# Loads of grouped keys and queries in pieces of 32 rows, in block 1's attention

## The chip, the cores and the metric

The kernel runs on one core of one Trainium2 chip. The metric is the device time of one execution in microseconds (us), as the median of several executions. Five engines work side by side, each through its own queue in order: TensorE (PE: matmuls, with the weight loads PEld), VectorE (DVE), ScalarE (ACT), GpSimd (POOL) and SyncE (SP), which in this stage issues all the loads and stores.

## The reference, cut to what matters

The program is a chain of three transformer blocks over 512 tokens of width 1024, all in float32. Only the first one's attention is touched. It has two kinds of heads: eight differential heads, whose query and key width is 32 twice over, and eight grouped-query heads of width 64, where four query heads share one key and value head.

```python
def gqa_attention(q, k, v):
    scale = d ** -0.5
    def block(qb):
        qg = qb.reshape(B, N_KV_B, GQA_GROUP, Q_BLOCK, d)
        s = jnp.einsum('bkgqd,bksd->bkgqs', qg, k) * scale
        p = jax.nn.softmax(s, axis=-1)
        o = jnp.einsum('bkgqs,bksd->bkgqd', p.astype(v.dtype), v)
...
qb = apply_rope(rms_norm(qb, q_norm), cos, sin)
kb = apply_rope(rms_norm(kb, k_norm), cos, sin)
ob = gqa_attention(qb, kb, vb)
x = x + jnp.concatenate([oa, ob], axis=-1) @ w_out
x = x + 0.5 * swiglu(rms_norm(x, ffn2_norm), ffn2_w_gate, ffn2_w_up, ffn2_w_down)
```

## The kernel before

All activations lie transposed: 128 partitions of features, 512 tokens in the free dimension. Float32 accuracy comes from splitting an operand into two parts, hi and lo, so a projection of 1024 x 128 weights is 24 matmuls of 128x512 (`mm3x`, L112; lines 116 to 118).

Block 1's attention is `heads1` (L559), called by `mix1` (L516). It runs the sixteen heads in an order written out by hand: differential head h, then grouped head h, for each chunk c of 0 to 3 and each r of 0 and 1. A head has four steps, one for each block of 128 queries. `attend` (L427) walks through all steps: in each it computes the scores and the exponentials of one step (`unit`, `soft`), turns and multiplies the weights of a step some way back (`values`, L455), and then takes one piece of "fill" (L724): a quarter of a projection for a later chunk (`proj_pieces`, L506), or, when those are used up, a piece of the first half of the output projection (`half_res`, L542). The fill keeps TensorE at work while DVE and ACT work on the softmax.

Queries and keys go through DRAM, because the heads need them in other partitions than the projection leaves them in. `parts` (L489) splits a projected chunk into hi and lo, and L500 stores both as one tile of 128 rows x 2 parts x 512 numbers (512 KB): `qdd` and `kdd` for the differential heads, `qpd` and `kpd` for the grouped ones. They are loaded back in three ways:

- `operand` (L614, load in L618) makes one stacked operand of a differential head: three loads of 32 partitions, 128 KB each, read as 32 rows by 2 heads. Tiles `qd` and `kd`.
- `keys` (L587, load in L592) makes the keys of a group of four heads: for the hi and the lo part one tile `kg`, of which both halves of 64 partitions get the same rows. That is four loads of 64 partitions, each read as 2 groups of 32 rows that lie 64 rows apart (`[(64, 2), (1, 32)]`).
- `ahead_gqa` (L683, load in L688) makes the queries of one grouped head: one tile `qg`, hi in the upper 64 partitions and lo in the lower, two loads of the same form.

`part_rows` (L503) writes the source's access pattern: row r and part i of such a tile begin at number 1024 r + 512 i, and each row read is 512 numbers long (2 KB).

The scores of a grouped head are two matmuls (L655): `qg` against the hi keys, then against the lo keys. Those of a differential head are one matmul for each of its two halves (L631).

`mk_diff` (L691) asks for the queries of the grouped head that follows, and `mk_gqa` (L695) for the operands of the differential head that follows, so each load is asked for about one head ahead. There are two buffers for `qg`, three for `kg` and four for `qd` and `kd` together. The order in which every engine gets its instructions is then worked out by a planner while the program is built (`schedule_with_timeline_sim=True` in `kernel`), from its own estimates of how long everything takes. SP issues its loads and stores in that order, and an issue that has to wait holds what is behind it.

Of the kernel before, what the change touches and what calls it, by code (L numbers as in the profile page):

```python
# [29 lines left out]
def f32v(ap):  # L30
    return ap.bitcast(F32)


class K:
    NU = 5
    SECOND = ("dq", "pf", "ct", "cacc")
    out = "out"
# [521 lines left out]
    def heads1(self, xhl, rb, gq, ind, ocs, rest):  # L559
        nc, D = self.nc, self.D  # L560
# [26 lines left out]
        def keys(kv):  # L587
            ds = []
            for i in range(2):
                t = self.keep("kg", 3, F32R)  # L590
                for r in range(2):
                    nc.sync.dma_start(out=f32v(t[64 * r:64 * r + 64]), in_=self.part_rows(gds[4], i, 32 * kv, [(64, 2), (1, 32)]))  # L592
                ds.append(t)
            return ds

# [65 lines left out]
        qds, kds, gds, ops = {}, {}, {}, {}  # L661
# [21 lines left out]
        def ahead_gqa(c, r):  # L683
            if r == 0 and c % 2 == 0:
                kg[c // 2] = keys(c // 2)
            t = self.keep("qg", 2, F32R)
            for i in range(2):
                nc.sync.dma_start(out=f32v(t[64 * i:64 * i + 64]), in_=self.part_rows(gds[c], i, 32 * r, [(64, 2), (1, 32)]))  # L688
            ops[4 + c, r] = t

        def mk_diff(c, r):  # L691
            ahead_gqa(c, r)
            return diff_head(2 * c + r, sms[c], *ops[c, r])
# [1434 lines left out]
```

## Time and profile before

| | us |
|---|---|
| median of 3 runs | 2696.18 (2693.70 to 2700.77) |
| the profiled execution, its own time | 2699.23 |
| its span, first to last instruction | 2697.5 |
| granted TensorE clock, mean over the span | 0.983 |
| block 1's attention, first load of an operand to last scores | about 404 to 681 |
| issues of `kg` (L592), 128 KB each | 8 |
| issues of `qg` (L688), 128 KB each | 16 |

In a row of the timeline stand the start and the length in us, the engine, the line, the operation, what it writes and reads, and in brackets how long the engine was idle before it and what ended that. "SPq" is SP's queue: its rows are the issues, not the transfers. In the chain of waits, a row such as "DMA kg<-kpd" is the time from an issue until what was waiting for the transfer went on. A row of the table by stages has the stretch, its length, the busy time of PE, PEld, DVE, ACT and POOL with the number of instructions, the granted clock of TensorE, the share of the 16 DMA engines' time that was busy, and GB/s.

### The profile page before, as it was taken

To read this page: it belongs to the slowest core of one execution; us is meant where nothing else is said; L and a number is where in the kernel's file an instruction comes from. 1 tells how busy PE (TensorE), PEld (TensorE's weight loads), DVE (VectorE), ACT (ScalarE), POOL (GpSimd) and SP (SyncE) were. 2 spreads that over 40 slices of the span, in tenths; PEclk is the share of its full clock that TensorE was granted. 3 is DMA by queue.
4 is the path that set the end of the run, shared out by engine and by line. 5 is a ranking of instruction groups with operands and counts; after the bars stand their busy time and mean duration, and the time that the engine had idled before them with its cause. 6 is when DMAs were issued, how large, how long until landed. Compare 5 with 4: busy or idle time off the path is not lost.

```text
span 2697.5 us, 31053 instructions
## 1 busy us (share of the span) xinstructions
PE 2606.5 (97%) x11752; PEld 2101.4 (78%) x11752; DVE 1579.3 (59%) x2435; ACT 1053.3 (39%) x1617; POOL 433.0 (16%) x343
## 2 busy tenths in 40 slices
PE   8999997899999999999999999999999899999999
PEld 6887785677788887888788877888778777878787
DVE  7866654777653554467434854434545977747464
ACT  4222234556422333455323443223433464424232
POOL 1011013433000001324111211000210313101000
PEclk9999998889999999999999999999999999999999
DMA  5566643334532233532223442222524634322333
GB/s 194 179 201 197 201 165 116 100 104 133 190 102 94 83 105 113 161 105 83 82 94 126 137 150 93 94 94 96 177 70 156 198 103 154 103 94 91 97 94 110
DMA packets 114449, 339.99 MB, mean 126 GB/s; under 512 B 13768, under 2 KB 15752, under 8 KB 114170
## 3 DMA queue, kind: packets, MB, share of 16 engines
q1 hardware_dynamic: 103866, 301.02, 34.4%
q0 software_dynamic: 10432, 36.97, 4.4%
q8 instruction: 92, 1.51, 0.2%
q14 instruction: 59, 0.48, 0.1%
HBM read 301.47 MB, written 40.67 MB: 127 GB/s over the span
## 4 chain that ended last, share of the span: by engine, by line
PE 87%; DVE 6%; DMA 4%; ACT 2%; issue 1%; POOL 0%; SPq 0%; DVEq 0%; POOLq 0%; ACTq 0%
PE b L118 5%; PE b L116 5%; PE b L117 5%; PE d L118 5%; PE d L116 5%; PE d L117 4%; PE f L116 4%; PE f L117 4%; PE f L118 4%; PE a L117 4%; PE a L118 4%; PE a L116 4%; PE c L116 4%; PE c L117 4%; PE c L118 4%; PE e L118 4%
## 5 line engine op out<-in xcount | busy, mean ns | idle before, releaser
L133 ACT ACTIVATE whi<-wraw 128x1024 fp32r<-128x1024 f32 (+3 forms) x419 | 423.7, 1014 | 1020.1 <-PE d L117 162.1
L134 DVE TENSOR_TENSOR wlo<-wraw,whi 128x1024 fp32r<-128x1024 f32 (+4 forms) x395 | 476.0, 1207 | 311.7 <-ACT whi L133 308.6
L116 PE MATMUL b<-xh,whi 128*128 128x512 f32 x360 | 141.9, 394 | 7.2 <-ACT xh L189 7.2
L118 PE MATMUL b<-xh,wlo 128*128 128x512 f32 x360 | 141.6, 393 | 0.4 <-DVE wlo L134 0.4
L117 PE MATMUL b<-xl,whi 128*128 128x512 f32 x360 | 141.8, 394 | 0.0
L118 PE MATMUL d<-xh,wlo 128*128 128x512 f32 x352 | 138.4, 393 | 2.0 <-DVE wlo L134 2.0
L116 PE MATMUL d<-xh,whi 128*128 128x512 f32 x352 | 138.6, 394 | 0.0
L117 PE MATMUL d<-xl,whi 128*128 128x512 f32 x352 | 138.0, 392 | 0.0
L118 PE MATMUL f<-xh,wlo 128*128 128x512 f32 x344 | 134.9, 392 | 0.6 <-DVE wlo L134 0.6
L116 PE MATMUL f<-xh,whi 128*128 128x512 f32 x344 | 135.2, 393 | 0.0
L117 PE MATMUL f<-xl,whi 128*128 128x512 f32 x344 | 134.3, 390 | 0.0
L186 ACT ACTIVATE hh<-h 128x512 fp32r<-128x512 f32 x98 | 61.8, 630 | 144.1 <-DVE h L365 92.6
L945 POOL TENSOR_TENSOR acc<-sq 128x512 f32<-128x512 f32 x10 | 14.1, 1410 | 641.1 <-ACT sq L292 375.8
L118 PE MATMUL e<-xh,wlo 128*128 128x512 f32 x288 | 112.9, 392 | 1.6 <-DVE wlo L134 1.6
L116 PE MATMUL e<-xh,whi 128*128 128x512 f32 x288 | 112.9, 392 | 0.0
L117 PE MATMUL c<-xl,whi 128*128 128x512 f32 x280 | 110.4, 394 | 2.6 <-DVE xl L190 2.6
L117 PE MATMUL e<-xl,whi 128*128 128x512 f32 x288 | 112.8, 392 | 0.0
L117 PE MATMUL a<-xl,whi 128*128 128x512 f32 x280 | 110.7, 395 | 2.0 <-DVE xl L190 2.0
L116 PE MATMUL a<-xh,whi 128*128 128x512 f32 x280 | 110.9, 396 | 0.0
L116 PE MATMUL c<-xh,whi 128*128 128x512 f32 x280 | 110.3, 394 | 0.3 <-ACT whi L133 0.3
L118 PE MATMUL a<-xh,wlo 128*128 128x512 f32 x280 | 110.2, 393 | 0.0
L118 PE MATMUL c<-xh,wlo 128*128 128x512 f32 x280 | 110.1, 393 | 0.0
(1178 smaller groups left out, 6510.2 us busy)
## 6 DMA issues: line engine op xcount, KB each, us to landing
wraw<-w_up SPq DMA_DIRECT2D x76, 512.0 KB
mw<-w_mod POOLq DMA_DIRECT2D x48, 512.0 KB, 4.5
wraw<-ffn_w_gate SPq DMA_DIRECT2D x43, 512.0 KB
wraw<-ffn_w_up SPq DMA_DIRECT2D x43, 512.0 KB
wraw<-w_down SPq DMA_DIRECT2D x40, 512.0 KB
wraw<-ffn_w_down SPq DMA_DIRECT2D x32, 448.0 KB
wraw<-w_gate SPq DMA_DIRECT2D x24, 512.0 KB
wraw<-ffn_w_down SPq DMA_DIRECT2D x16, 512.0 KB
```

The costliest lines, as they stand in the source:

```text
L116: mm(out, ah, bh, start=(first and i == 0), stop=False)
L117: mm(out, ah, bl, start=False, stop=False)
L118: self.last_mm = mm(out, al, bh, start=False, stop=(last and i == n - 1)).ins
L133: nc.scalar.activation(hi[:, i:j], raw[:, i:j], AF.Copy)
L134: (nc.gpsimd if self.pool_lo else nc.vector).tensor_sub(lo[:, i:j], raw[:, i:j], f32v(hi[:, i:j]))
L186: nc.scalar.activation(hi, x, AF.Copy)
L945: i = (self.nc.vector if c == 6 else self.nc.gpsimd).tensor_add(a, acc, s).ins
```

## The change

Each load of 64 partitions is cut into two of 32 partitions, which read the two groups of 32 rows one by one. The same bytes go to the same places. The 8 loads of `kg` become 16 and the 16 of `qg` become 32, of 64 KB each. The stores, the operand loads of the differential heads, the buffers and all the computation stay as they are.

```diff
@@ keys
                 t = self.keep("kg", 3, F32R)
                 for r in range(2):
-                    nc.sync.dma_start(out=f32v(t[64 * r:64 * r + 64]), in_=self.part_rows(gds[4], i, 32 * kv, [(64, 2), (1, 32)]))
+                    for a in range(2):
+                        nc.sync.dma_start(out=f32v(t[64 * r + 32 * a:64 * r + 32 * a + 32]), in_=self.part_rows(gds[4], i, 32 * kv + 64 * a, [(1, 32)]))
                 ds.append(t)
@@ ahead_gqa
             t = self.keep("qg", 2, F32R)
             for i in range(2):
-                nc.sync.dma_start(out=f32v(t[64 * i:64 * i + 64]), in_=self.part_rows(gds[c], i, 32 * r, [(64, 2), (1, 32)]))
+                for a in range(2):
+                    nc.sync.dma_start(out=f32v(t[64 * i + 32 * a:64 * i + 32 * a + 32]), in_=self.part_rows(gds[c], i, 32 * r + 64 * a, [(1, 32)]))
             ops[4 + c, r] = t
```

## The prediction

> **What bounds the kernel now.** I read the page first, then the table by stages over block 1's attention, then TensorE's waits there, and last the DMA queue's own order. The page's head:
>
> ```profile
> span 2697.5 us, 31053 instructions
> ...
> PE 2606.5 (97%) x11752; PEld 2101.4 (78%) x11752; DVE 1579.3 (59%) x2435; ACT 1053.3 (39%) x1617; POOL 433.0 (16%) x343
> ```
>
> TensorE is busy 97% of the span, so only the holes in its work can be won. Two stages of 62 and 58 us around the end of the attention (columns: length, busy time of PE, PEld, DVE, ACT, POOL, then the granted clock, the DMA share of 16 engines, GB/s):
>
> ```profile
> 570.00:632.00 62.00, 54.46 (x269) 42.76 (x268) 45.82 (x109) 37.95 (x83) 19.50 (x15) 0.89 0.31 90
> 632.00:690.00 58.00, 55.26 (x294) 42.07 (x292) 44.42 (x105) 36.88 (x82) 19.21 (x14) 1.00 0.38 124
> ```
>
> From 632 on PE is busy 55.26 of 58 us at clock 1.00, although DVE and ACT do as much there as in the 62 us before. The work pushed behind the attention's steps is a fixed amount, so an idle microsecond saved before 632 should come out at the end nearly whole. The holes that a DMA ends, from the timeline of PE (in brackets the idle time before it):
>
> ```profile
> 453.54 0.76 PE L655 MATMUL a<-kg,qg 128*128 128x512 f32 x1 [5.29 <-DMA kg<-kpd]
> 458.75 0.47 PE L655 MATMUL a<-kg,qg 128*128 128x512 f32 x1 [1.13 <-DMA kg<-kpd]
> 498.84 0.77 PE L631 MATMUL a<-kd,qd 96*128 96x512 f32 x1 [5.59 <-DMA kd<-kdd]
> 559.84 0.77 PE L631 MATMUL a<-kd,qd 96*128 96x512 f32 x1 [3.42 <-DMA qd<-qdd]
> 625.16 0.76 PE L631 MATMUL a<-kd,qd 96*128 96x512 f32 x1 [4.85 <-DMA qd<-qdd]
> ```
>
> These five waits are 5.29 + 1.13 + 5.59 + 3.42 + 4.85 = 20.28 us, and the table of waits lists no others there that a transfer ends for PE. I call them place 1 (453.54 and 458.75), place 2 (498.84), 3 (559.84) and 4 (625.16). Only place 1 names a tile that the change touches; places 2 to 4 wait for operands of the differential heads. What links them is in the chain of waits and in SP's queue (start, length, what):
>
> ```profile
> 441.65 4.14 DMA kpd<-hl
> 447.42 11.19 DMA kg<-kpd
> 484.62 6.72 DMA kdd<-hl
> 549.43 6.47 DMA kdd<-hl
> 557.32 2.51 DMA qd<-qdd
> 612.51 8.81 DMA kdd<-hl
> ```
>
> ```profile
> 445.80 6.97 SPq L592 DMA_DIRECT2D kg<-kpd  x6
> 478.72 1.04 SPq L688 DMA_DIRECT2D qg<-qpd  x2
> 485.53 0.50 SPq L688 DMA_DIRECT2D qg<-qpd  x1
> 491.40 1.26 SPq L618 DMA_DIRECT2D kd<-kdd  x3
> 494.11 4.34 SPq L618 DMA_DIRECT2D kd<-kdd  x3
> 541.98 1.04 SPq L688 DMA_DIRECT2D qg<-qpd  x2
> 555.96 1.26 SPq L618 DMA_DIRECT2D kd<-kdd  x3
> 607.11 1.04 SPq L688 DMA_DIRECT2D qg<-qpd  x2
> 621.34 1.26 SPq L618 DMA_DIRECT2D kd<-kdd  x3
> ```
>
> At places 2 to 4 the chain goes back through the operand loads to the store `kdd`, which takes 6.72, 6.47 and 8.81 us to land. Each of these stores stands behind two loads of `qg` in SP's order (478.72, 541.98, 607.11), and the `kd` loads of place 2 behind a third (485.53). The DMA share says why that matters; five stretches, the last with nothing but operand loads of 32 rows:
>
> ```profile
> 449.00:459.00 10.00, 4.33 (x11) 3.24 (x12) 0.00 (x0) 1.65 (x2) 0.45 (x1) 0.83 0.13 50
> 488.60:492.00 3.40, 3.40 (x14) 2.75 (x13) 0.51 (x1) 0.60 (x1) 0.00 (x0) 0.65 0.13 51
> 553.20:556.40 3.20, 2.99 (x14) 2.26 (x14) 2.03 (x4) 2.21 (x8) 0.00 (x0) 1.00 0.11 44
> 616.00:620.50 4.50, 3.33 (x15) 2.11 (x13) 3.02 (x6) 2.08 (x6) 0.00 (x0) 1.00 0.13 51
> 622.70:625.20 2.50, 0.04 (x1) 0.07 (x1) 0.00 (x0) 0.00 (x0) 0.00 (x0) 0.78 0.93 261
> ```
>
> In 449 to 459 only the `kg` loads run: share 0.13 at 50 GB/s. Two of 16 engines are 0.125, so one load of 64 rows (131 KB) runs on two engines and takes 131/50 = 2.6 us; four take 10.5, which is the 11.19 us of the chain at place 1. The same share appears as a tail at places 2 (488.6 to 492.0), 3 (553.2 to 556.4) and 4 (616.0 to 620.5): 14 engines have finished, and the store waits for its share on the two that the `qg` loads have filled. The operand loads, whose outermost extent is 32 on both sides, run at 0.93.
>
> **The change part by part.** 24 loads (8 of `kg`, 16 of `qg`) become 48 with the same bytes, each 32 rows on both sides. This trace has none of exactly that form. The nearest rows are the old loads and the operand loads (min, median, max ns of one issue):
>
> ```profile
> L592 SPq DMA_DIRECT2D kg<-kpd x8: 475/499/2443, 445.8 to 559.2; - x8
> ```
>
> ```profile
> L688 SPq DMA_DIRECT2D qg<-qpd x16: 474/496/879, 427.9 to 626.4; - x16
> ```
>
> ```profile
> L618 SPq DMA_DIRECT2D kd<-kdd x24: 302/423/536, 406.3 to 625.0; - x24
> ```
>
> *Issue.* I take 0.42 us from L618, the same outermost 32 rows; the other end is 0.50 from L592. SP goes from 24 x 0.50 = 12.0 to 48 x 0.42 = 20.2 us, 8.2 more over some 200 us. Behind the added issues at places 2 to 4 stand first-operand loads and the `kdd` store; I cost this at nothing, because between 485.53 and 491.40 and in the like gaps SP waits for that store. If that cover is gone, it is two issues, 0.84 us, at each of three places, 2.5 us.
>
> *Landing.* One operand load landed 2.51 us after its issue (557.32 above); I take that for a piece, although a piece has half the bytes. The far end is 4.14, a 512 KB store with little beside it (441.65).
>
> *Place 1.* The stored keys land at 445.80 and the loads start. The first operand becomes four pieces: the fourth starts 3 x 0.42 later, at 447.06, and lands at 449.6. PE then starts 3.9 us sooner than 453.54. The second operand's last piece is the eighth: 445.80 + 7 x 0.42 + 2.51 = 451.25. PE has 4.1 us of work between its two waits, to 453.7, so the 1.13 goes too: 5.0 together; 3.4 with 4.14 as landing.
>
> *Place 2.* With no two-engine queue ahead of it the store should land as the undisturbed one did, 484.62 + 4.14 = 488.76. From the first load of a group of three to PE's start pass 3.85 us (555.96 to 559.84 and 621.34 to 625.16 are 3.88 and 3.82), so the operands are there at 492.7, before PE runs dry at 498.84 - 5.59 = 493.25. All 5.6 us go. At the low end the store keeps its 6.72 us, and only 491.40 to 498.84 (7.44) shrinks to 3.85: 3.6 us.
>
> *Place 3.* 549.43 + 4.14 = 553.57 instead of 555.90: 2.3 us, the rest of the wait stays. Low end 0, if the store's own writing sets it.
>
> *Place 4.* By 616.0 the other 14 engines were done. The two `qg` loads, spread out, add 262 KB / 16 = 16 KB to each engine, 0.65 us at 25 GB/s; landing followed the tail's end by 0.8. So 617.5 instead of 621.3: 3.8 us.
>
> The sum of the waits is 5.0 + 5.6 + 2.3 + 3.8 = 16.7, between 3.4 + 3.6 + 0 + 3.8 = 10.8 and 20.3.
>
> *Clock.* After each of the four places PE runs at clock 0.50 (first 453.5 to 456.9, 3.40 us; the other three 6.80 us; columns as above):
>
> ```profile
> 497.80:504.60 6.80, 5.76 (x18) 4.84 (x19) 3.07 (x8) 2.60 (x6) 0.91 (x1) 0.50 0.48 141
> ...
> 624.10:630.90 6.80, 5.74 (x16) 4.61 (x17) 2.67 (x7) 2.75 (x6) 1.25 (x1) 0.50 0.53 125
> sum 23.80, PE 21.13 PEld 17.09 DVE 8.78 ACT 8.87 POOL 3.92; mean PE 5.28 PEld 4.27 DVE 2.19 ACT 2.22 POOL 0.98
> ```
>
> At full clock the 21.13 busy us would take half, so at most 10.6 are to be had. They are not all mine: a shorter gap was followed by half clock too, with 1.5 us of idle PE in 2.6,
>
> ```profile
> 485.00:487.60 2.60, 1.07 (x3) 0.68 (x4) 2.46 (x5) 1.95 (x6) 0.00 (x0) 1.00 0.85 302
> 487.60:491.00 3.40, 3.40 (x11) 2.73 (x10) 0.39 (x2) 0.30 (x3) 0.00 (x0) 0.50 0.38 124
> ```
>
> and places 1, 3 and 4 keep 1.0 to 1.4 us of idleness. I take a third, 3.5 us, between 0 and 10.6. The Trainium skill, TensorE: Matmul & The Clock Gate, Part 1, puts the drop after an idle window of about 3.4 us; by that, no wait that is left would bring it, and the sum would be 27 us. The trace speaks against it with the row above.
>
> Together 16.7 + 3.5 = 20.2 us. The profiled execution took 2699.23 us for its span of 2697.5 and lies 3.05 above the median of the runs, 2696.18; taken off that median it gives 2676. The order of all instructions is worked out by a planner from its own estimates; a load that it moves can give or take one such wait, up to 5.6 us, which the range holds.
>
> **The rivals.** *The stores are slow by themselves.* Then only place 1 (5.0) and the loads of place 2 (3.6) gain: 8.6 us, 2687.6. For it: writing 512 KB took 4.14 us even undisturbed. Against it: tails at 0.11 to 0.13 before each landing. Chance 0.15.
>
> *The pieces still go to two engines*, or what they free is hidden anyway: the same bytes at the same 50 GB/s, about 2696. Against it stands the 0.93 of loads with 32 rows outermost. The Trainium skill, DMA: Bandwidth & Descriptors, Why a DMA increments its semaphore by 16 and not by 1, gives the number of engines as the largest up to 16 that divides the outermost extents of both sides: 2 for 64 and 2, 16 for 32 and 32. The trace agrees as to the first, 0.13. Chance 0.09.
>
> *Slower: the pieces pay one after another.* SP takes its queue in order, and an issue can be held until an unrelated load has landed:
>
> ```profile
> SPq L618 <- DMA qg<-qpd: 4.7, 2, 3.1
> ```
>
> One `kg` issue took 2.443 us, and three `kd` issues at 494.11 took 4.34. If every piece waits 2.51 us for the one before, place 1's eight end at 445.80 + 20.1 = 465.9, 7.1 us later than now. At place 4 four query pieces take 10 us instead of 1.04; with the three operand loads between, the store starts 6.0 us later, at 618.5, and lands 4.14 later, 1.4 after today's 621.3. At places 2 to 4 alike that is 7.1 + 3 x 1.4 = 11.3 us: 2707.5. It decides from a spacing of (12.95 - 2.51)/7 = 1.5 us between pieces, where place 1 breaks even. Against it: operand loads stand 0.42 us apart in groups of three. The Trainium skill, DMA: Bandwidth & Descriptors, Rules for kernel authors, speaks for this outcome: it advises one large transfer over several small ones, and says that transfers to disjoint partition halves serialize on the same engines. Its ground, that both halves already use all 16, is not what the 0.13 shows. Chance 0.09.
>
> **How the numbers follow.** The forecast has 0.67. Its own range goes from 2696.2 - 30.9 (all waits and all of the clock) to 2696.2 - 10.8: 2665 to 2685. To hold the time 8 times in 10 the range takes in the first rival and a little for the planner: 2664 to 2690. What a measurement of this kernel can tell from no change is about 0.3%, 8.1 us, so faster means below 2688.1. Faster is 0.66 from the forecast and 0.09 from the first rival, 0.75; the same is 0.06 of the first, 0.08 of the second and 0.01 each of forecast and third, 0.16; slower 0.01 and 0.08, 0.09.
>
> **What would show it.** In the profile after, 48 issues at L593 and L690 of about 0.42 us; no stretch at share 0.13 after a store; `kdd` landing in 3 to 5 us; PE's DMA waits in the attention down from 20.3 to about 4 us; two or three half-clock stretches fewer; and from 632 on the same work, some 20 us earlier. The forecast is wrong if the tails at 0.13 remain (second rival), if they go and the stores still take 6 to 9 us (first), or if SP's issues of pieces last 1.5 us and more (third).

## The result, and the profile after

The changed kernel takes 2664.12 us (median of 4 executions, 2662.76 to 2667.01) against 2694.94 us of the kernel before (2690.91 to 2700.77). The ratio is 0.9885, with a 95% interval of 0.9865 to 0.9906: 31 us less, between 25 and 36. A ratio below 1 is faster. A second set of four executions gave 2667.23 us (expected 2662 to 2667), 0.9898 (0.9884 to 0.9913), and in its profile no hole is left in the attention that a DMA ends. The forecast was 2676, 20 us less, with a range of its own from 2665 to 2685; 2664.12 lies just under it.

The head of the page of the changed kernel:

```profile
span 2665.2 us, 31091 instructions
...
PE 2592.2 (97%) x11752; PEld 2090.8 (78%) x11752; DVE 1582.3 (59%) x2435; ACT 1051.9 (39%) x1617; POOL 431.8 (16%) x343
```

The span is 32.3 us shorter. PE's busy time went from 2606.5 to 2592.2 us with the same 11752 matmuls, 14.3 less, and its idle time from 2697.5 - 2606.5 = 91.0 to 2665.2 - 2592.2 = 73.0, 18.0 less. Both happened in the attention. The table by stages, from 425 us to the first load of the next block's context (688.02 before, 654.89 after), first of the kernel before, then of the changed one:

```profile
425.00:688.02 263.02, 225.15 (x1063) 172.17 (x1064) 182.00 (x423) 149.83 (x325) 93.91 (x65) 0.90 0.35 109
```

```profile
425.36:654.89 229.53, 210.09 (x1063) 161.33 (x1064) 184.88 (x423) 148.67 (x325) 93.89 (x65) 0.96 0.40 125
```

Same 1063 matmuls, 33.5 us less: 15.1 us less of busy time at a mean clock of 0.96 in place of 0.90, and 18.4 us less idleness (263.02 - 225.15 = 37.87, and 229.53 - 210.09 = 19.44). All of the gain arises here, and 32.3 of the 33.5 us are still there at the end.

The holes that a DMA ended were 20.28 us. In the changed kernel's timeline of PE only one is left. (From here on a line's number can be one to five higher than in the kernel before, where the edit added lines above it.)

```profile
483.86 0.47 PE L632 MATMUL a<-kd,qd 96*128 96x512 f32 x1 [1.16 <-DMA kd<-kdd]
```

The keys' and queries' loads (min, median, max ns of one issue):

```profile
L593 SPq DMA_DIRECT2D kg<-kpd x16: 317/419/423, 444.0 to 538.8; - x16
```

```profile
L690 SPq DMA_DIRECT2D qg<-qpd x32: 317/419/737, 428.3 to 596.1; - x32
```

SP's queue around the four places. The time from a store's row to the row of the load behind it is the store's landing:

```profile
441.42 0.32 SPq L500 DMA_DIRECT2D kpd<-hl  x1
444.03 5.42 SPq L593 DMA_DIRECT2D kg<-kpd  x12
475.67 0.34 SPq L500 DMA_DIRECT2D kdd<-hl  x1
478.70 1.27 SPq L619 DMA_DIRECT2D kd<-kdd  x3
531.71 0.34 SPq L500 DMA_DIRECT2D kdd<-hl  x1
534.66 1.26 SPq L619 DMA_DIRECT2D kd<-kdd  x3
586.13 0.32 SPq L500 DMA_DIRECT2D kdd<-hl  x1
590.61 1.26 SPq L619 DMA_DIRECT2D kd<-kdd  x3
```

The three `kdd` stores land after 3.0, 3.0 and 4.5 us, before it was 6.72, 6.47 and 8.81. The key store at 441.42 also lands sooner, after 2.6 us where it was 4.14. While the keys come in, PE no longer stops (stretch, length, busy time of PE, PEld, DVE, ACT, POOL, clock, DMA share, GB/s):

```profile
446.00:450.00 4.00, 4.00 (x25) 3.48 (x24) 1.29 (x2) 1.69 (x3) 0.17 (x1) 1.00 0.51 143
```

The share is 0.51 and not 0.13, and PE is busy 4.00 of 4 us. The first scores with the new keys start at 449.88 without a wait.

### The profile page after: what moved, and what is told of

It is laid out like the page before. It is cut to its first block, busy times and chain, and to the rows that moved or that the text cites. A ratio compares the mean times of both kernels' runs of the same rounds, so it can differ in the third digit from the quotient of the medians.

```text
span 2665.2 us, 31091 instructions
## 1 busy us (share of the span) xinstructions
PE 2592.2 (97%) x11752; PEld 2090.8 (78%) x11752; DVE 1582.3 (59%) x2435; ACT 1051.9 (39%) x1617; POOL 431.8 (16%) x343
## 4 chain that ended last, share of the span: by engine, by line
PE 79%; issue 8%; DVE 6%; DMA 3%; ACT 2%; POOL 1%; SPq 0%; POOLq 0%; DVEq 0%; ACTq 0%
PE d L118 4%; PE d L116 4%; PE b L118 4%; PE f L116 4%; PE d L117 4%; PE f L117 4%; PE b L116 4%; PE b L117 4%; PE f L118 4%; PE a L118 4%; PE a L117 4%; PE a L116 4%; PE c L116 3%; PE c L117 3%; PE c L118 3%
```

## The experiments

My theory is that of the forecast: a load whose outer extent (the count of its slowest dimension) is 2 runs on two DMA engines, and what stands behind it on those two is late. It has two rivals. A: smaller pieces land earlier, whatever engines they use. B: the planner's other order of instructions brought the gain. All ratios are to the kernel before on the same chip, with their 95% intervals.

**Whole loads, other order of reading** (twice). The two dimensions of the source change places; the loads stay whole. Queries and keys get the same permuted order of features, so the scores are the same sums. Every engine's instructions stand in the order of the kernel before.

```diff
-in_=self.part_rows(gds[4], i, 32 * kv, [(64, 2), (1, 32)])
+in_=self.part_rows(gds[4], i, 32 * kv, [(1, 32), (64, 2)])
...
-in_=self.part_rows(gds[c], i, 32 * r, [(64, 2), (1, 32)])
+in_=self.part_rows(gds[c], i, 32 * r, [(1, 32), (64, 2)])
```

> The 24 loads stay whole, 64 partitions each, but the source is read with the 32 rows as the outer extent and the two groups as the inner one, for keys and queries alike (both get the same permuted order of rows, so the scores are the same sums). Every engine's instructions stand in the same order as in the kernel before. Theory (a load whose outer extent is 2 on one side runs on two DMA engines, and what is behind it on those two waits): outer extents 32 and 64 use all 16, no stretch at a DMA share of 0.13, the kdd stores land in 3 to 4.5 us, PE's DMA waits in the attention 20.3 -> under 2 us, time 2660 to 2670. Rival A (smaller pieces land earlier, whatever engines they use): nothing is cut, so about 2695. Rival B (the planner's other order brought the gain): the order is that of before, so about 2695.

> The 24 whole loads with 32 rows as the outer extent once more, beside the others of this set: does the form without added issues beat the changed kernel? It saves 24 issues, of which two stand ahead of the first scores at place 1 (0.8 us). Theory: 2662 to 2668, not to be told from the changed kernel.

Measured: 2666.29 us, 0.9902 (0.9885 to 0.9919), and 2662.78 us, 0.9876 (0.9861 to 0.9891). The gain comes with no load cut and no instruction moved. This settles it against both rivals: neither the size of the pieces nor the planner's order is needed, only the outer extent. The second run's loads, a stretch in which only keys are loaded, and what PE still waits for in the attention (total us, times, longest):

```profile
L592 SPq DMA_DIRECT2D kg<-kpd x8: 518/594/597, 442.9 to 536.3; - x8
```

```profile
445.00:448.50 3.50, 3.50 (x22) 3.01 (x21) 1.29 (x2) 1.09 (x2) 0.00 (x1) 1.00 0.63 186
```

```profile
PE a L631 <- DMA kd<-kdd: 0.8, 1, 0.8
```

A share of 0.63 is the full time of ten engines, so more than eight are at work. This form needs 24 issues and not 48, but one takes 0.59 us and not 0.42. From the changed kernel (0.9885 and 0.9898) it can't be told apart.

**Pieces on 2, 4, 8 and 16 engines.** The 48 pieces of the change, but with their 32 rows read in two dimensions (2 by 16, 4 by 8, 8 by 4, 16 by 2), again alike for queries and keys. The four kernels have one and the same order of instructions on every engine.

```diff
-32 * kv + 64 * a, [(1, 32)])
+32 * kv + 64 * a, [(1, 2), (2, 16)])      # or (1, 4), (4, 8); (1, 8), (8, 4); (1, 16), (16, 2)
...
-32 * r + 64 * a, [(1, 32)])
+32 * r + 64 * a, [(1, 2), (2, 16)])
```

> The 48 loads of 32 partitions of the changed kernel, but each reads its 32 rows as 2 outer by 16 inner (rows 0, 2, 4 ... and then 1, 3, 5 ..., for keys and queries alike). Theory: each piece runs on two engines, 64 KB in 1.3 us; the tails at share 0.13 are back, PE waits about 20 us for DMAs, time 2690 to 2705, as before or a little slower for the 24 issues more. Rival A (smaller pieces by themselves): 2660 to 2670, as the changed kernel. Rival B (the planner's order): between, since its order is near that of the changed kernel: 2664 to 2680.

> The 48 pieces with their 32 rows read as 4 outer by 8 inner. Theory: four engines each, DMA share 0.25 where they run alone, 64 KB in 0.65 us at 100 GB/s; a query's tail is a quarter of that before, so most of the waits go: PE waits 2 to 6 us for DMAs, 2668 to 2678. If the count of engines did not matter, as with two engines, 2690 to 2700; if any count over two were as good as 16, 2662 to 2667.

> The 48 pieces with their 32 rows read as 8 outer by 4 inner. Theory: eight engines, 64 KB in 0.33 us, which is less than the 0.42 us of an issue, so nothing queues: 2662 to 2669, PE waits under 2 us.

> The 48 pieces with their 32 rows read as 16 outer by 2 inner: 16 engines. Every engine's instructions stand in the same order as in the kernels with 2, 4 and 8 engines, which is another order than that of the changed kernel. It tells the engines apart from the planner's order. If 16 engines are worth more than 8: 2664 to 2668, as the changed kernel. If the planner's order costs the rest: 2672 to 2677, as with 8 engines, and 8 us of the changed kernel's lead over those forms belong to its order.

| outer extent | median us | ratio | PE's DMA waits in the attention, us |
|---|---|---|---|
| 2 | 2695.89 | 1.0009 (1.0001 to 1.0018) | 18.7 |
| 4 | 2680.99 | 0.9951 (0.9936 to 0.9966) | 4.3 |
| 8 | 2675.23 | 0.9928 (0.9915 to 0.9942) | 1.6 |
| 16 | 2671.34 | 0.9918 (0.9901 to 0.9935) | 0.9 |

A stretch of each, in that order, in which only keys are loaded:

```profile
450.50:458.00 7.50, 5.76 (x32) 4.62 (x31) 1.29 (x2) 2.74 (x4) 2.04 (x1) 1.00 0.13 46
```

```profile
449.50:455.00 5.50, 5.50 (x32) 4.68 (x30) 1.29 (x2) 2.13 (x4) 0.33 (x1) 1.00 0.24 80
```

```profile
446.00:452.00 6.00, 6.00 (x31) 4.87 (x30) 1.46 (x3) 3.05 (x5) 1.44 (x2) 1.00 0.32 94
```

```profile
449.00:454.50 5.50, 5.50 (x33) 4.69 (x31) 1.29 (x2) 2.74 (x4) 0.93 (x2) 1.00 0.35 104
```

Shares of 0.13 and 0.24 are 2 and 4 of 16 engines. At 8 and 16 the share is 0.32 and 0.35, because the issues set the pace: one takes 0.59 to 0.65 us in this form, and 64 KB (65.5 thousand bytes) in that time are 101 to 111 GB/s, near the 94 and 104 GB/s of the rows. So these two shares do not tell the number of engines. Cutting alone gains nothing (first row). Between 8 and 16 the intervals overlap. By its ratio the form with 16 by 2 lies 5 to 9 us behind the changed kernel (0.9898 and 0.9885), though the intervals overlap; it differs from it in the planner's order and in the length of an issue, and which of the two costs that, if it is real, was not tried. The waits came out as expected in all three forms with a number for them. The times with 4 and 8 engines, 2680.99 and 2675.23 us, are misses: I had expected at most 2678 and 2669. With 16 the time falls between the two outcomes that I had named, so it does not decide between them.

The waits of the first row, and the chain's stores there:

```profile
PE a L632 <- DMA kd<-kdd: 13.2, 2, 12.4
PE a L656 <- DMA kg<-kpd: 5.5, 2, 3.7
```

```profile
482.22 7.74 DMA kdd<-hl
551.45 7.65 DMA kdd<-hl
```

The stores are slow again, 7.74 and 7.65 us.

**One of the two edits alone.** Only the first hunk of the change (keys), and only the second (queries).

> Only the loads of the keys are cut into pieces of 32 rows; the queries stay in loads of 64 on two engines. Theory: place 1 goes (6.4 us of waiting and the two half-clock stretches of 3.4 us behind it, some 2 to 3 us of PE time), the tails behind the query loads and the waits of places 2 to 4 stay: 2685 to 2689. Rival A and the changed kernel's gain shared by bytes (8 of 24 loads): a third of 31, 2685; rival B: anywhere between 2664 and 2695.

> Only the loads of the queries are cut into pieces of 32 rows; the keys stay in loads of 64 on two engines. Theory: places 2 to 4 go with the half clock behind them, place 1 stays (keys wait 6.4 us): 2671 to 2675. Rival A (by bytes, 16 of 24 loads): two thirds of 31, 2674, but with waits left at all four places. Rival B: anywhere between 2664 and 2695.

Keys alone: 2683.83 us, 0.9970 (0.9956 to 0.9985). Queries alone: 2669.30 us, 0.9912 (0.9898 to 0.9926). So 8 and 24 us, in sum the change. Both lie 1 to 2 us below the ranges that I had named. The waits, keys alone first:

```profile
PE a L632 <- DMA kd<-kdd: 9.4, 2, 6.8
PE a L632 <- DMA qd<-qdd: 4.9, 1, 4.9
PE a L656 <- DMA kg<-kpd: 0.2, 1, 0.2
```

```profile
PE a L655 <- DMA kg<-kpd: 3.9, 2, 3.5
```

With the keys cut, the waits for differential operands are all there (14.3 us); with the queries cut, they are gone, although their loads and stores are untouched. By SP's queue the three `kdd` stores take 6.4, 6.0 and 8.6 us to land with the keys cut, and 3.0, 2.9 and 4.3 with the queries cut. The keys wait 3.9 us there and not the 6.4 that I had expected to stay: their store too lands sooner, after 2.6 us in place of 4.14. That is the queue on the two engines, seen from both sides.

**Twice as many pieces.** 96 loads of 16 rows on 16 engines.

```diff
-for a in range(2):
+for a in range(4):
-    ...t[64 * i + 32 * a:64 * i + 32 * a + 32]), in_=self.part_rows(gds[c], i, 32 * r + 64 * a, [(1, 32)]))
+    ...t[64 * i + 16 * a:64 * i + 16 * a + 16]), in_=self.part_rows(gds[c], i, 32 * r + 64 * (a // 2) + 16 * (a % 2), [(1, 16)]))
```

> The same bytes in 96 loads of 16 rows, on 16 engines each (32 KB a load). It prices the issues. Theory: at 0.42 us an issue the first keys' operand at place 1 waits for eight issues in place of four, 1.7 us, and the second for sixteen, 3.4 us; elsewhere the issues fit into SP's waits: 2665 to 2672. If pieces paid one after another (2.5 us each), it would be 2690 or more.

Measured: 2671.68 us, 0.9910 (0.9897 to 0.9923), within what was expected. Even 72 issues more than before do not make the loads pay one after another.

**Keeping PE busy in the waits.** The kernel before, with matmuls whose results are dropped ahead of the first scores of each place. The diff shows those of places 2 to 4; place 1 has 20 of the same kind in `gqa_head`, with a projection's operand.

```diff
 p = self.psum("scores")
+for _ in range({2: 22, 4: 13, 6: 19}.get(h, 0) if q == s == 0 else 0):
+    nc.tensor.matmul(p, vraw[4][:, :128], vraw[4][:, :512], start=True, stop=True)
 self.last_score = nc.tensor.matmul(p, q2[:96, s, ...], k2[:96, s], start=True, stop=True).ins
```

> The kernel before, with all its loads on two engines, and 74 matmuls of 128x512 more whose results are thrown away: 20, 22, 13 and 19 of them ahead of the first scores at places 1 to 4, a little less than fits into the waits at 0.23 us each. The DMA waits stay, but PE is busy in them. Theory (half clock follows stretches of low PE business, and it is what the forecast priced too low): the half-clock stretches behind the four places go, mean clock 0.983 to 0.986 -> 0.989 to 0.991, and the time falls by 5 to 10 us, to 2684 to 2689, although the waits are all there. Rival (the clock is worth little, since other engines set the pace in those stretches): 2692 to 2698, or slower where the added matmuls come out of place.

Measured: 2706.91 us, 1.0044 (1.0029 to 1.0059). As a whole a miss: the planner put the added matmuls of places 1 to 3 ahead of other work and not into those waits. They cost their time, and the waits stayed:

```profile
PE a L634 <- DMA qd<-qdd: 14.0, 2, 12.4
PE a L660 <- DMA kg<-kpd: 7.0, 2, 4.2
```

Only at place 4 did they come near where they were meant to. PE's timeline there:

```profile
624.77 4.48 PE L633 MATMUL a<-vt 128*128 128x512 f32 x19
...
633.15 0.47 PE L634 MATMUL a<-kd,qd 96*128 96x512 f32 x1 [1.60 <-DMA qd<-qdd]
```

The store still took 8.1 us (621.13 to 629.21 in SP's queue), and all but 1.60 us of the wait was filled. From the first scores to the context load, of the kernel before, of this one and of the changed one:

```profile
625.16:688.02 62.86, 60.35 (x310) 46.98 (x311) 46.96 (x107) 39.04 (x86) 20.48 (x15) 0.95 0.38 121
```

```profile
633.15:692.00 58.85, 57.56 (x306) 44.29 (x307) 47.62 (x107) 39.16 (x87) 20.30 (x15) 1.00 0.41 130
```

```profile
594.33:654.89 60.56, 57.96 (x310) 45.08 (x311) 48.01 (x107) 39.16 (x87) 20.45 (x15) 1.00 0.40 126
```

With PE kept busy the clock stayed at 1.00, and the stretch took 58.85 us in place of 62.86. The work in it is nearly the same: eight small matmuls of 128x2 (0.8 us) come only behind the context load there, and four others (0.6 us) are in it instead. Of the 4.0 us, 2.8 are less busy time and 1.2 less idleness. In the changed kernel the same stretch, with the same 310 matmuls, is 2.3 us shorter, and its busy time is 2.4 less. So the clock is worth some 2.5 us at this one place, a little less than half of the 5.74 busy us that I had counted in the half-clock stretch there.

## Why the forecast was right in its mechanism and too small

- **What carries it.** Two engines for a load with an outer extent of 2, and the stores and operands behind it in their queues: right. Whole loads with 32 as the outer extent gain it all; pieces with 2 gain nothing.
- **Issues and landing.** For an issue 0.42 us taken, 0.419 measured. The added ones cost nothing that could be seen, as forecast. For a piece's landing 2.51 us taken; from issue to landing the pieces of `kg` took 1.9 us in the median, 3.0 at most.
- **Place 1.** The scores start at 449.88, forecast 449.6 after a wait. That these agree is luck. No wait is left, because the key store too lands 1.5 us sooner and the loads start at 444.03 and not at 445.80; PE has other work until 449.88.
- **Places 2 to 4.** The store's landing was set at 4.14, the "undisturbed" row. It was not undisturbed. Four query loads are issued at 427.93 in the kernel before, and up to the issue of the key store at 441.65 two engines' worth of transfers is still running; in the changed kernel the DMA share of the same stretch is 0.00:

```profile
440.00:442.00 2.00, 1.99 (x6) 1.49 (x7) 2.00 (x4) 1.77 (x4) 0.00 (x0) 0.50 0.13 51
```

  In the changed kernel the landing is 2.6 to 3.0 us, and 4.5 at place 4, where a weight load is issued 0.58 us ahead of the store; whether that is why was not tried. So place 3, for which 1.1 us of waiting was left in the forecast, has none. Waits in all: forecast 16.7, measured 20.28 - 1.16 = 19.1, and 18.0 of all idle time.
- **The clock, the step that failed:** "I take a third, 3.5 us, between 0 and 10.6." Measured in the two profiles, PE's busy time fell by 14.3 us for the same matmuls. In this pair the term was four times too small, and its upper end fell short too. The sentence that only the holes in PE's work can be won does not hold either: 14.3 of the 32.3 us came out of its busy time. Two things were wrong in the term. Only the 23.8 us behind the four places were counted; in 425 to 690 the kernel before has ten stretches of half clock, 51.2 us, and the changed one three, 17.1. And two thirds of the half clock were expected to stay behind gaps of 1.0 to 1.5 us; none of the three stretches that are left (from 435.1, 459.0 and 506.8 on) stands behind a wait of the four places. The lost ones include stretches at 487.6 and 586.6, behind gaps that no DMA ends. Part of that is chance: the gap of 1.7 us before 584.98 is there in the changed kernel too (1.75 us before 561.04), this time with no half clock behind it, and a second profile of the changed kernel has five stretches, 23.9 us.
- **How much of it is the change.** The profiled execution of before was one with many such stretches: 0.983, where 43 timed executions average 0.9850. Eight of the changed kernel average 0.9896. The difference is 0.0046 x 2 x 2680 = 25 us of half clock, at most 12 us of time; by the 1.8 us for each 0.001 of the last section it is 8. With 18 us of idleness that makes 26 to 30, which fits the two sets (ratios 0.9885 and 0.9898, 31 and 27 us). So some 8 to 12 us of the clock are the change's, two to three times the 3.5 of the forecast; this is worked out from averages, and only at place 4 was it tried by itself. The 2.5 us there are most of what the forecast gave the clock in the whole stage. What the clock is worth at places 1 to 3 by itself stays open.
- **The rivals.** Slow stores: they land in 3.0 to 4.5 us, not 6 to 9. Still two engines: the share is 0.51, and two would give 0.125. One after another: issues 0.42 us apart, and 96 loads still gain.

The Trainium skill, DMA: Bandwidth & Descriptors, Why a DMA increments its semaphore by 16 and not by 1, gives the engines as the largest number up to 16 that divides both outer extents. The rows agree for 2 and 4 (0.13 and 0.24); for the pieces on 8 and 16 the issue hides it, and the whole loads' 0.63 shows no more than that it is over 8. The advice in its Rules for kernel authors, not to split a transfer into disjoint partition halves, does not hold where the whole one runs on two engines; the whole form with another order of reading obeys both.

## What to carry to other kernels

Look at the DMA share in a stretch where one kind of load runs alone: 0.13 is two engines of sixteen, and the cure may be as small as exchanging two dimensions of the access pattern. Such a load costs most where it is not waited for: the stores and loads queued behind it on those engines are late, and the waits bear their names. When PE's waits go, count the half-clock stretches of the whole stage, not only those behind the waits, and in more than one profile.

## What the runs showed of the hardware

The clock follows how busy PE was in the stretch of 3.41 us before, on a fixed grid of such stretches. I laid that grid over 300 to 700 us of thirteen profiles and took PE's busy share from the table by stages. At full clock, 41 of 41 stretches under 0.45 were followed by half clock, 39 of 123 between 0.45 and 0.75, and 1 of 1207 above. At half clock, 28 of 29 under 0.85 stayed there, and 83 of 98 above came back. So a gap of 1 to 2 us can cost a stretch, depending on how it lies on the grid. The Trainium skill, TensorE: Matmul & The Clock Gate, Part 1, speaks of an idle window; by these counts one that is more than 55% idle was enough each time, and one that is 25 to 55% idle in 39 of 123 cases. This also goes with more than half of the variance between executions of one kernel: over the 116 whose clock is recorded, compared within each kernel, a mean clock lower by 0.001 went with 1.8 us more (correlation -0.79).
